# First products on a tile of ones, the sample's narrow products joined into longer turns, and the last unit's scaling on VectorE, in a streaming encoder layer

## The chip, the cores and the metric

The kernel runs on one core of one Trainium2 chip. The core's engines are TensorE (PE, matrix products; its weight loads are shown as PEld), VectorE (DVE), ScalarE (ACT), GpSimd (POOL) and SyncE (SP), which here only starts transfers. The metric is the device time of one execution in microseconds (us).

## The reference

One layer of an encoder is applied to two groups of rows that share all weights: a prompt of 2048 rows and a sample of 32 rows (the next frames of a running stream), each row of 1024 numbers, all in float32.

```python
h = rmsnorm(x, g_pre_mix)
z = h @ w_in                                  # 1024 -> 2560: u | q | f | i | g
u_ext = concatenate([pool_hist, u])           # mixer A: trailing means over 2, 4, 8, 16 frames
y_pool = einsum('blgc,gcd->blgd', d, w_pool) * pool_scale
S1, o = hgrn_run(S0, silu(zq), kin, zi, logf) # mixer B: 4 heads of 128, a gated recurrence
y_hg = rmsnorm(o, g_hg_norm) * silu(zg)
x = x + rmsnorm(concatenate([y_pool, y_hg]) @ w_out, g_post_mix)
h2 = rmsnorm(x, g_pre_ffn)
f = (silu(h2 @ w_gate) * (h2 @ w_up)) @ w_down   # 1024 -> 2816 -> 1024
x = x + rmsnorm(f, g_post_ffn)
```

Outputs are both groups' rows, and for each group the last 15 rows of u and the recurrence's final state.

## The kernel before

**Stages.** The prompt is worked on in two halves of 1024 rows; the second half carries the sample with it. For each half come the value columns (`first_values` for the first half, `values` for the second), four heads (`head_products`, with the recurrence in the generator `hgrn`), four pool columns (`pool_products`), the output projection (`project`, with `post` behind it), and gate and up (`gate_up`). When both halves are through, `down` makes the last product for both and writes the rows.

**Products.** A prompt product is made from parts in a rounded format: each operand is split into a high and a low part, and three products of 128x512 (high by high, high by low, low by high) are added up in one bank of PSUM. Twelve such products make one channel tile of four row tiles in `value_products`, or one slot in gate and up and in down, which use a seven-product scheme of two-by-two blocks. There are eight banks: four in the pool `mm` and four in the pool `ax`.

**Sample products.** The sample's 32 rows are multiplied in plain float32, with the sample as the stationary operand: 32 columns wide, so that four products stand side by side in the four column quarters of the array, and the k-th part of the sum goes to the quarter k mod 4. A product of four quarters is turned and summed by one more product with a 0/1 matrix (columns `C_I4` of the constants). The profile shows every plain float32 product as two records. Three kinds matter here:

- `fps`, in `sample_tile` (L618): eight products for one column tile of w_in, 16 records. They are issued as soon as the tile's weights are taken, ahead of the tile's prompt products; 5 us later by the planner's clock the copy `fst` is turned.
- `gb`, in `group` inside `hgrn` (L709): the small products within chunks of the recurrence, also 32 columns wide, in six groups for each head.
- `gsps`, in `sampled` (L1217): 16 products for one matrix tile pair of gate or up (32 records), issued right after product 6 of that tile. Even m is gate, odd m is up; a gate and an up tile share a bank, which `sample_hidden` (L1122) copies whole to `sT`, turns by four products `zps` with 32 columns, and multiplies to the hidden sample rows.

**Order.** PE's order is the order in which the code issues its products, with small tasks put in between: a `Task` holds a generator and a time on a counter (`Pace.t`) that every product advances by an estimate; `poll` steps each task whose time has come. In `gate_up` and `down` the slots are listed by `order_of`. Other engines' orders are made by a scheduler from the dependences. In `gate_up`, raw weight tiles (`wraw`) are loaded about nine slots ahead of use; `drop` frees a tile when its last part has been formed and, in the second half, when its sample products are made. A load that wants a buffer waits for that in SP's queue.

**The start.** `first_values` (L517) loads x by channels and the weights of the value columns. ScalarE forms the scaled high part `xg` (L532) and rounds the weights to `whw` (L213); VectorE forms the low parts (L533, L214). The first pass over the second row group uses the unscaled rows; `token_stats` (L422) computes for each row tile a sum of squares (ACT, L288), the reciprocal root (POOL, L294 and L295) and a diagonal matrix `dg` (POOL, L429), which `scaled_channels` (L449) multiplies with a matrix of ones into `rb`, for the second pass.

**The end.** In `down`, `half_done` (L1457) is called when one half (512 columns) of a row tile's sum is complete: square sum (ACT), scaling by g_post_ffn, and, after the second half, the reciprocal root. `done` finishes the row tile and stores it. For the very last unit (`direct`, row tiles 11 and 15) POOL multiplies three of the four halves by g_post_ffn (L1474), DVE the fourth (`fg`, L1471), DVE scales by the root and adds the residual (L1487), and stores go by SP and ACT queues.

## Time and profile before

| | us |
|---|---|
| median of 3 runs (lowest to highest) | 2156.44 (2155.46 to 2156.99) |
| the profiled execution's own time | 2157.55 |
| its span in the trace | 2155.7 |
| PE busy in the span | 2131.6 |
| DVE, ACT, POOL busy | 1426.7, 822.8, 286.3 |

The profile is one execution. The page gives busy time per engine, groups of instructions by line, and what ended the idle time before them; the list of waits says who waited for whom; the time-ordered view prints each instruction with its start and length from the span's start. Since products are pipelined, a 128x512 product is shown 0.39 us long although the next starts 0.23 us after it: cost is read from start to start.

### The profile page before, as it was taken

Reading aid. Unit: us, or ns where it says so; the run is one execution under the profiler, and the core shown is the slowest. Engines: PE = TensorE matmul, PEld = TensorE weight load, DVE = VectorE, ACT = ScalarE, POOL = GpSimd, SP = SyncE. Lnnn points to the kernel's source line nnn. Section 1 sums busy time; section 2 is a strip of 40 time slices with the busy share of each in tenths; the row PEclk is TensorE's granted clock in tenths of the full one; section 3 lists DMA queues with packets and bytes.
Section 4 is the critical chain, followed back from the end, with each engine's and each line's share of the span. In section 5 each row is a group of like instructions: output and inputs, shape, how many; then the busy total and the mean of one; then the engine's idle time right before and its main releaser. Section 6 shows DMA issues by size and latency. Waiting matters only on the chain.

```text
span 2155.7 us, 34195 instructions
## 1 busy us (share of the span) xinstructions
PE 2131.6 (99%) x13196; PEld 1702.8 (79%) x13196; DVE 1426.7 (66%) x2321; ACT 822.8 (38%) x1604; POOL 286.3 (13%) x391
## 2 busy tenths in 40 slices
PE   8999999999999999999999999999999999999998
PEld 6788778888888887777777788888888777877876
DVE  5655665787776777465574687766667756466587
ACT  6434345554444444233323564444434521011032
POOL 2233301100000010122220210000000211110134
PEclk9999999999999999999999999999999999999999
DMA  8121134445545559011004624544454796776778
GB/s 312 50 70 41 40 128 156 127 117 167 160 144 156 147 161 291 20 44 42 17 23 159 198 81 125 149 137 143 137 150 139 233 324 194 225 222 192 220 214 211
DMA packets 388783, 316.16 MB, mean 147 GB/s; under 512 B 16007, under 2 KB 318335, under 8 KB 388622
## 3 DMA queue, kind: packets, MB, share of 16 engines
q1 hardware_dynamic: 386318, 306.37, 46.6%
q0 software_dynamic: 2016, 7.34, 1.8%
q8 instruction: 104, 1.70, 0.3%
q14 instruction: 57, 0.47, 0.1%
q10 hardware_dynamic: 288, 0.28, 0.0%
HBM read 215.56 MB, written 98.37 MB: 146 GB/s over the span
## 4 chain that ended last, share of the span: by engine, by line
PE 89%; DVE 4%; ACT 1%; issue 1%; POOL 1%; DMA 1%; SPq 0%; DVEq 0%; POOLq 0%; ACTq 0%
PE gx L176 21%; PE mmb L176 15%; PE gy L176 11%; PE dx L176 10%; PE ops L176 9%; PE dy L176 5%; PE gz L176 5%; PE dz L176 2%; PE vps L176 2%; PE gb L176 1%; PE gsps L176 1%; PE gw L176 1%; PE ups L176 1%; DVE acc L1455 1%; PE pps L176 1%
## 5 line engine op out<-in xcount | busy, mean ns | idle before, releaser
L176 PE MATMUL gx<-fhi,wf 128*128 128x512 f32 x1376 | 447.5, 394 | 0.0
L176 PEld LDWEIGHTS gx<-fhi,wf 128*128 128x128 f32 x1376 | 258.4, 188 | 60.0 <-issue 1.0
L176 PE MATMUL gx<-flo,wf 128*128 128x512 f32 x688 | 269.8, 392 | 0.0
L176 PE MATMUL gy<-fhi,wf 128*128 128x512 f32 x704 | 232.8, 393 | 0.0
L176 PE MATMUL mmb<-hThi,whi 128*128 128x512 f32 x512 | 219.3, 428 | 0.0
L176 PE MATMUL dx<-dhi,hst 128*128 128x512 f32 x640 | 213.4, 394 | 0.4 <-DVE acc L1455 0.3
L176 PE MATMUL mmb<-hThi,wlo 128*128 128x512 f32 x512 | 201.8, 394 | 0.0
L176 PE MATMUL mmb<-hTlo,whi 128*128 128x512 f32 x512 | 201.6, 394 | 0.0
L1455 DVE TENSOR_TENSOR acc<-dx,acc 128x512 f32<-128x512 f32 x168 | 115.2, 689 | 77.1 <-PE dx L176 76.3
L1189 DVE TENSOR_TENSOR wf<-s,wf 128x512 fp32r<-128x512 f32 x176 | 120.4, 687 | 65.9 <-ACT wf L1184 63.1
L176 PEld LDWEIGHTS gy<-fhi,wf 128*128 128x128 f32 x704 | 132.1, 188 | 30.7 <-issue 0.2
L176 PEld LDWEIGHTS gx<-flo,wf 128*128 128x128 f32 x688 | 129.4, 188 | 28.4
L1184 ACT CAST wf<-s 128x512 fp32r<-128x512 f32 x176 | 108.2, 621 | 104.9 <-PE gy L176 34.9
L176 PEld LDWEIGHTS dx<-dhi,hst 128*128 128x128 f32 x640 | 120.1, 188 | 32.5 <-issue 3.4
L176 PE MATMUL gy<-flo,wf 128*128 128x512 f32 x352 | 137.9, 392 | 0.0
L176 PE MATMUL dx<-dlo,hst 128*128 128x512 f32 x320 | 125.8, 393 | 0.0
L1189 DVE TENSOR_TENSOR wf<-wraw,wf 128x512 fp32r<-128x512 f32 x132 | 89.5, 687 | 45.9 <-ACT wf L1184 45.7
L176 PEld LDWEIGHTS mmb<-hThi,whi 128*128 128x128 f32 x512 | 96.7, 189 | 25.2 <-issue 6.4
L176 PEld LDWEIGHTS mmb<-hThi,wlo 128*128 128x128 f32 x512 | 96.4, 188 | 22.4
L176 PE MATMUL dy<-dhi,hst 128*128 128x512 f32 x320 | 112.9, 393 | 0.3 <-DVE acc L1455 0.3
L1184 ACT CAST wf<-wraw 128x512 fp32r<-128x512 f32 x132 | 80.7, 621 | 82.5 <-PE gz L176 23.5
L176 PEld LDWEIGHTS mmb<-hTlo,whi 128*128 128x128 f32 x512 | 96.9, 189 | 18.5 <-issue 2.6
(332 smaller groups left out, 4102.9 us busy)
## 6 DMA issues: line engine op xcount, KB each, us to landing
hst<-hdFalse SPq DMA_DIRECT2D x140, 256.0 KB, 3.0
hst<-hdTrue SPq DMA_DIRECT2D x140, 256.0 KB, 3.1
wraw<-in_w_gate_dram SPq DMA_DIRECT2D x50, 512.0 KB, 4.2
wraw<-in_w_up_dram SPq DMA_DIRECT2D x50, 512.0 KB, 4.2
hdFalse<-hhi SPq DMA_DIRECT2D x77, 256.0 KB, 2.3
hdFalse<-hlo SPq DMA_DIRECT2D x77, 256.0 KB, 2.5
hdTrue<-hhi SPq DMA_DIRECT2D x77, 256.0 KB, 2.5
hdTrue<-hlo SPq DMA_DIRECT2D x77, 256.0 KB, 3.3
```

What stands on the lines that cost most here:

```text
L176: nc.tensor.matmul(out, l, r, start=start, stop=stop, skip_group_check=more)
L1184: nc.scalar.copy(wf[:, 0], getattr(M, src) if isinstance(src, str) else src)
L1189: nc.vector.tensor_tensor(wf[:, 1], getattr(M, src) if isinstance(src, str) else src, wf[:, 0].bitcast(F32), ALU.subtract)
L1455: nc.vector.tensor_tensor(dst, ps, dst, ALU.add)
```

## The change

1. `first_values` begins with a tiny activation on ACT and 12 products of a tile of ones by itself into a spare bank, which nothing reads.
2. The first channel tile's 12 products are ordered high by high, low by high, high by low over all four row tiles, instead of the three for each row tile in turn.
3. `token_stats` can do some of its row tiles; the first row group's four are done two and two in the second pass. `dg` is formed by DVE instead of POOL.
4. `sample_tile` becomes a task that begins 6.5 us later by the planner's clock, or when `join` calls it: `group` calls `join` just ahead of its own products, so that `fps` stands beside `gb`.
5. `sampled` takes a list. For gate tiles from m = 6 on, the sample products of gate and up are issued together after the gate tile's product 5 (after product 6 of the up tile for the last pair); the first six tiles are as before. The two matrix parts of a tile now share 128 columns of the bank (two quarters each), so that the copy is 256 wide instead of 512, and two products with 64 columns (constants `C_PAIR`) turn it instead of four with 32.
6. In the last unit DVE multiplies all four halves by g_post_ffn and POOL does both root steps; row tile 15 is finished one slot after its sum, and each row tile's second half is stored by ACT's queue.
7. The square sums of the second half's rows (`later_stats`) start 20 us later by the planner's clock.

The diff, cut to its core:

```diff
+    c[:, C_PAIR:C_END] = ((q[:, None] == r[None, :] // NS) & (s[:, None] == r[None, :] % NS)).astype(np.float32)
...
+        def token_stats(S, tg, tiles=range(4)):
...
-                nc.gpsimd.tensor_scalar(S.dg[tg][:, i], ident, S.rs[tg][i], None, ALU.mult)
+                nc.vector.tensor_scalar(S.dg[tg][:, i], ident, S.rs[tg][i], None, ALU.mult)
...
+            idle = small("idle", [P, 1], bufs=1)
+            nc.scalar.activation(idle, ones[:, 0:1], AF.Copy)
+            bank = axbank("idle")
+            for _ in range(12):
+                mm(bank[:, 0:P], ones, ones, True, True, 0.0)
...
-                    for i in range(4):
-                        value_products(pss, i, ah, al, i * P, hi[kk], lo[kk], k + kk == 0, k + kk == KD - 1)
+                    if k + kk == 0:
+                        for n, (a, b) in enumerate(((ah, hi[0]), (al, hi[0]), (ah, lo[0]))):
+                            for i in range(4):
+                                mm(pss[i], a[:, i * P:(i + 1) * P], b, n == 0, False, rcost(512))
+                    else:
...
                 if k == 2:
+                    token_stats(S, 0, range(2))
                     next(later, 0)
                 elif k == 4:
-                    token_stats(S, 0)
+                    token_stats(S, 0, range(2, 4))
...
-            ps = axbank("fps")
-            for k in range(KD):
-                q = k % 4
-                mm(ps[32 * q:32 * q + 32, 0:P], S.hsr[:, k, :], raw[:, k * P:(k + 1) * P], k < 4, k >= 4, 60.0)
-
-            def rest():
+
+            def whole():
+                task.begun = True
+                ps = axbank("fps")
+                for k in range(KD):
+                    q = k % 4
+                    mm(ps[32 * q:32 * q + 32, 0:P], S.hsr[:, k, :], raw[:, k * P:(k + 1) * P], k < 4, k >= 4, 60.0)
...
-            return Task(rest())
+            task = Task(whole(), 6500.0)
+            task.begun = False
+            Pace.joint.append(task)
+            return task
+
+        def join():
+
+            for tk in Pace.joint:
+                if not tk.begun:
+                    tk.step()
+            Pace.joint.clear()
...
             def group(goff, src, pick, n=16):
+                join()
...
-            st = t2("sT")
-            nc.vector.tensor_copy(st, sps)
+            st = t2("sT", [P, 2, P])
+            nc.vector.tensor_copy(st, sps[:, 0:2 * P].rearrange("p (m c) -> p m c", c=P))
...
-            for c in range(4):
-                mm(zps[:, c * NS:(c + 1) * NS], st[:, c * P:(c + 1) * P], cons[:, C_I4:C_I4 + NS], True, True, 215.0)
+            for c in range(2):
+                mm(zps[:, c * 2 * NS:(c + 1) * 2 * NS], st[:, c], cons[:, C_PAIR:C_END], True, True, 215.0)
...
-                    sampled(m, M)
+                    if m < LEAD or m == len(mats) - 1:
+                        sampled([m] if m < LEAD else [m - 1, m])
...
+                    if LEAD <= m < len(mats) - 2 and m % 2 == 0:
+                        sampled([m, m + 1])
...
-                if direct and dh == 1 and t == units[-1][2] + 8:
+                if direct:
                     fg = t2("fg")
                     nc.vector.tensor_tensor(fg, f, gpf[0][:, cs], ALU.mult)
-                    stats[t].append(fg)
-                elif direct:
-                    nc.gpsimd.tensor_tensor(f, f, gpf[0][:, cs], ALU.mult)
+                    stats[t].append((dh, fg))
...
-                    rstd_of(st, P, True, nc.vector if direct else nc.gpsimd, dh)
-                    pending.append((slot[0] + (0 if direct else 4), lambda: done(t, direct)))
+                    rstd_of(st, P, True, nc.gpsimd, dh)
+                    pending.append((slot[0] + (1 if direct else 4), lambda: done(t, direct)))
...
-                    Task(later_stats(halves[1]), 5000.0)
+                    Task(later_stats(halves[1]), 25000.0)
```

Three places in the orders. First PE in the first head of the second half, at the gate column's sample products: `fps` are the column tile's products, `mmb` the prompt's, `gb` the chunk products. Before:

```order
L176 MATMUL fps<-wraw,hsr 32x128 x8
L176 MATMUL mmb<-hThi_7375,whi 128x512
L176 MATMUL mmb<-hTlo_7376,whi 128x512
L176 MATMUL mmb<-hThi_7375,wlo 128x512
L176 MATMUL mmb<-hThi_7377,whi 128x512
L176 MATMUL mmb<-hTlo_7378,whi 128x512
L176 MATMUL mmb<-hThi_7377,wlo 128x512
L176 MATMUL mmb<-hThi_7379,whi 128x512
L176 MATMUL mmb<-hTlo_7380,whi 128x512
L176 MATMUL mmb<-hThi_7379,wlo 128x512
L176 MATMUL gb<-q_t,k_t 32x16 x33
```

And now:

```order
L180 MATMUL mmb<-hTlo_7395,whi 128x512
L180 MATMUL mmb<-hThi_7394,wlo 128x512
L180 MATMUL fps<-wraw,hsr 32x128 x8
L180 MATMUL gb<-q_t,k_t 32x16 x33
L180 MATMUL mmb<-hThi_7396,whi 128x512
```

The column tile's products have moved behind nine prompt products, to the edge of the chunk products. Of 16 column tiles eight stand beside a `gb` now, one before (another stood beside the value columns' sample products `vsps` before, and no longer does).

Second PE in gate and up of the second half, at a gate tile of the steady part: `gx` are prompt products, `gsps` the sample's. Before, after the gate tile's product 6:

```order
L176 MATMUL gx<-fhi,wf 128x512 x2
L176 MATMUL gx<-flo,wf 128x512
L176 MATMUL gx<-fhi,wf 128x512
L176 MATMUL gsps<-wraw,hs_11306 32x128 x16
L176 MATMUL gz<-fhi,wf 128x512
```

And now, after its product 5:

```order
L180 MATMUL gx<-fhi,wf 128x512 x2
L180 MATMUL gx<-flo,wf 128x512
L180 MATMUL gx<-fhi,wf 128x512
L180 MATMUL gsps<-wraw,hs_11321 32x128 x32
L180 MATMUL gx<-fhi,wf 128x512
```

The up tile's 16 products have come to the gate tile's. In all, turns of 32-column products on PE (one or more of `fps`, `gb`, `gsps` and the others in a row) are 96 before and 82 now.

Third DVE at the end: `acc` are the row sums, `dx`, `dy`, `dz` banks of the last unit's products, `fg` the halves multiplied by g_post_ffn (`gv`), `x1r` the residual. Before:

```order
L1455 TENSOR_TENSOR acc<-dz,acc 128x512
L1490 SCALAR_TENSOR_TENSOR acc<-acc,st,gv 128x512
L1455 TENSOR_TENSOR acc<-dy,acc 128x512
L1455 TENSOR_TENSOR acc<-dx,acc 128x512
L1455 TENSOR_TENSOR acc<-dy,acc 128x512
L1455 TENSOR_TENSOR acc<-dx,acc 128x512
L292 TENSOR_SCALAR st<-st 128x1
L1471 TENSOR_TENSOR fg<-acc,gv 128x512
L1487 SCALAR_TENSOR_TENSOR acc<-acc,st,x1r 128x512 x2
L292 TENSOR_SCALAR st<-st 128x1
L1487 SCALAR_TENSOR_TENSOR acc<-acc,st,x1r 128x512
L1487 SCALAR_TENSOR_TENSOR acc<-fg,st,x1r 128x512
```

And now:

```order
L1526 SCALAR_TENSOR_TENSOR acc<-acc,st,gv 128x512
L1509 TENSOR_TENSOR fg<-acc,gv 128x512
L1493 TENSOR_TENSOR acc<-dy,acc 128x512
L1493 TENSOR_TENSOR acc<-dx,acc 128x512
L1509 TENSOR_TENSOR fg<-acc,gv 128x512
L1493 TENSOR_TENSOR acc<-dy,acc 128x512
L1509 TENSOR_TENSOR fg<-acc,gv 128x512
L1493 TENSOR_TENSOR acc<-dx,acc 128x512
L1523 SCALAR_TENSOR_TENSOR acc<-fg,st,x1r 128x512
L1509 TENSOR_TENSOR fg<-acc,gv 128x512
L1523 SCALAR_TENSOR_TENSOR acc<-fg,st,x1r 128x512 x3
```

A product `fg` has come ahead of the first add of `dy`, two more stand between the adds, and the two small root steps have left DVE for POOL.

More of the change, by code (lines that the diff above doesn't have):

```diff
@@ L44 @@
 C_VEC = C_I4 + NS
-C_END = C_VEC + 32
+C_PAIR = C_VEC + 32
+C_END = C_PAIR + 2 * NS
 NPAIR = NJ // 2
@@ L116, in body @@
         w_down = ins["w_down"][0]
-        vec = cons[:, C_VEC:C_END]
+        vec = cons[:, C_VEC:C_PAIR]
         g_pre, g_ffn, p_scale, g_hg = vec[:, 0:8], vec[:, 8:16], vec[:, 16:20], vec[:, 28:29]
@@ L170, in body @@
             tasks = []
+            joint = []
         def tick(ns):
@@ L1142, in gate_up @@
                 S.hsm = ztile("hsm", [P, NJ, NS])
-            jobs, later = [], []
+            jobs, later, gs = [], [], {}
             def load(m, p):
@@ L1486, in done @@
                     if direct:
-                        nc.vector.scalar_tensor_tensor(f[:, ds], fg[0] if fg and i else f[:, ds], rs, xh[:, ds], ALU.mult, ALU.add)
-                        (nc.scalar if fg and i else nc.sync).dma_start(out=outs[0][0, rows, ds], in_=f[:, ds])
+                        nc.vector.scalar_tensor_tensor(f[:, ds], dict(fg)[i], rs, xh[:, ds], ALU.mult, ALU.add)
+                        (nc.scalar if i else nc.sync).dma_start(out=outs[0][0, rows, ds], in_=f[:, ds])
                     else:
```

42 lines of the change are left out of this document (25 added, 17 removed).

## The prediction

> **What bounds the kernel now.** I read the profile page first, then the list of waits of TensorE, then the time-ordered view of the first 30 us, of one turn of each kind of sample product, and of the last 15 us. The first fence is the busy line of the page and two rows of the waits (engine, operation waited with, releaser: us in total, times, longest).
>
> ```profile
> PE 2131.6 (99%) x13196; PEld 1702.8 (79%) x13196; DVE 1426.7 (66%) x2321; ACT 822.8 (38%) x1604; POOL 286.3 (13%) x391
> ...
> PE vps L176 <- ACT whw L213: 6.8, 1, 6.8
> PE rb L176 <- POOL dg L429: 1.1, 1, 1.1
> ```
>
> TensorE (PE) is busy for 2131.6 of 2155.7 us. Of the 24.1 us left, 6.85 are the wait for the first weights, some 10 lie behind the last product, and the largest other wait that the change touches is 1.1 us. So the time is the length of the queue of products, plus its two ends. A change pays if it shortens that queue or one of the ends, and costs if it opens a new wait in the queue. Other engines matter only there.
>
> **The start.** First half of the time-ordered view (start, length, engine, line, operation, out<-in, count, idle before).
>
> ```profile
> 0.77 0.20 POOL L137 MEMSET ones<- 128x128 f32 x1
> ...
> 4.27 1.28 ACT L532 ACT_TABLE_LOAD   x1 [4.27 <-DMA xT<-x_channels]
> ...
> 6.20 1.12 ACT L213 CAST whw<-wrow 128x512 fp32r<-128x512 f32 x2
> ...
> 6.85 0.79 PE L176 MATMUL vps<-whw,xg 128*128 128x512 f32 x1 [6.85 <-ACT whw L213]
> ...
> 12.16 1.00 PE L176 MATMUL vps<-whw,xg 128*128 128x512 f32 x2
> ...
> 13.00 0.39 PE L176 MATMUL vps<-wlw,xg 128*128 128x512 f32 x1
> 13.23 0.63 PE L176 MATMUL vps<-whw,xg 128*128 128x512 f32 x2
> ...
> 20.86 0.19 ACT L288 ACTIVATION_READ_ACCUMULATOR junk<-xt 128x1 f32 x1
> ...
> 26.58 1.05 PE L176 MATMUL rb<-dg,ones 128*128 128x128 f32 x8
> ...
> 27.39 0.47 PE L176 MATMUL vps<-whw,xg 128*128 128x512 f32 x1
> ```
>
> Two products from 12.16 to 13.00 are 0.42 us each; from 13.00 to 13.23 one takes 0.23. So the first 6 us of products run at half rate, and then the full rate is granted. From 6.85 to the rb products at 26.58 stand six channel tiles of 12 products, 72 in 19.73 us; at 0.23 they would take 16.6, so 3.1 us are lost to the slow beginning.
>
> The change puts 12 products of a tile of ones (24 records) ahead. They can start when that tile is set, at about 1.0. The eight rb records take 0.81 us (26.58 to 27.39), 0.10 each; at half rate 0.20, so 24 end at about 5.9. The table load also moves from 4.27 to the idle activation at about 1.2, so the first weight cast could start 1.28 earlier, at 4.9, if its data were there; they landed at 6.20 at the latest. The first real product therefore falls between 5.6 and 6.85; I take 6.1, just behind the idle ones. With full rate from there, rb comes at 6.1 + 16.6 = 22.7 instead of 26.58: 3.9 us. I take off 0.4 for a rest at half rate: **3.5 us**, between 1.5 (the rate rises late) and 4.2. The Trainium skill, page "TensorE: Matmul & The Clock Gate", section "What's actually happening", says that the full rate needs one busy window of about 3.4 us and that these windows run freely. The trace agrees as far as it can: 6 us of half rate lie within one to two windows. By that rule the full rate would come anywhere from 4.4 to 7.8, at worst 1.7 us of half rate after 6.1, which costs 0.9 instead of my 0.4.
>
> The new order of the first 12 products (four with the low weight part last) only takes away the need for wlw as the second operand. The square sums that feed the first rb stay where the landing of their rows puts them; the last ends at 21.05, and two POOL steps (the longer, the power, takes 0.54 in a row of the end below) and dg on VectorE (DVE) then end at about 22.2, just ahead of rb at 22.7. If they came later, they would take from the 3.5. In the second pass two of four sums are brought forward, and dg no longer queues on POOL, so the 1.1 us wait of the second rb should go: **1.1**, between 0 and 1.1.
>
> **The sample products.** Three kinds of turn of PE in the second half. In each fence stand the last full product ahead, the turn, and the two products behind it (one in the third). First a turn of the gate and up products, 32 records; then a turn of one column tile, 16 records; then the one place where a column tile already stands beside the chunk products (gb).
>
> ```profile
> 1279.58 0.39 PE L176 MATMUL gx<-fhi,wf 128*128 128x512 f32 x1
> 1279.90 1.08 PE L176 MATMUL gsps<-wraw,hs 128*32 128x128 f32 x32
> 1280.91 0.50 PE L176 MATMUL gx<-fhi,wf 128*128 128x512 f32 x1
> 1281.24 0.39 PE L176 MATMUL gx<-flo,wf 128*128 128x512 f32 x1
> ```
>
> ```profile
> 881.71 0.39 PE L176 MATMUL mmb<-hThi,wlo 128*128 128x512 f32 x1
> 882.02 0.64 PE L176 MATMUL fps<-wraw,hsr 128*32 128x128 f32 x16
> 882.60 0.50 PE L176 MATMUL mmb<-hThi,whi 128*128 128x512 f32 x1
> 882.93 0.39 PE L176 MATMUL mmb<-hTlo,whi 128*128 128x512 f32 x1
> ```
>
> ```profile
> 907.72 0.39 PE L176 MATMUL mmb<-hThi,wlo 128*128 128x512 f32 x1
> 908.04 0.77 PE L176 MATMUL gb<-qa,k_t 128*32 128x16 f32 x66
> 908.71 0.64 PE L176 MATMUL fps<-wraw,hsr 128*32 128x128 f32 x16
> 909.29 0.51 PE L176 MATMUL mmb<-hThi,whi 128*128 128x512 f32 x1
> ```
>
> Cost of a turn: from the product ahead to the second behind, less two products of 0.23. For 32 records 1281.24 - 1279.58 - 0.46 = 1.20; for 16 records 882.93 - 881.71 - 0.46 = 0.76. So a record is 0.0275 us and a turn has a fixed 0.32 to 0.34 us whatever it holds: 0.08 more ahead, 0.10 behind, the rest while the array empties. Eight pairs (seven in the steady part, and the last) now hold 64 records in one turn instead of twice 32: 8 x 0.34 = **2.7 us**, at least 8 x 0.18 = 1.4 if only the two edges go.
>
> In the order of PE, turns of narrow products fall from 96 to 82: these eight, and six column tiles fewer that stand alone (14 before, 8 now). In the last fence gb goes into fps without an edge: fps still takes 0.58 to the next product as it does alone. So a join saves the edges, 0.18, and up to 0.34 if one emptying goes as well. I take 0.2: 6 x 0.2 = **1.2**, up to 2.0.
>
> The turn of the sample's hidden rows, now four products with 32 moving columns (8 records):
>
> ```profile
> 1290.50 0.97 PE L176 MATMUL zps<-cons,sT 128*128 128x32 f32 x8
> 1291.31 0.48 PE L176 MATMUL gy<-fhi,wf 128*128 128x512 f32 x1
> ```
>
> 0.81 us for 8 records, 0.10 each, as much as an rb record with 128 columns. So width does not set it up to 128, and four records with 64 columns take 0.40: 11 pairs x 0.405 = **4.5**. The trace has no record of 64 columns; if each took twice as long nothing would be gained, but the rb row speaks for 4.5.
>
> **The end.** The last operations (the last product of all starts at 2145.28).
>
> ```profile
> 2142.63 0.50 PE L176 MATMUL dy<-dhi,hst 128*128 128x512 f32 x1 [0.34 <-DVE acc L1455]
> ...
> 2144.33 0.69 DVE L1455 TENSOR_TENSOR acc<-dy,acc 128x512 f32<-128x512 f32 x1 [0.96 <-PE dy L176]
> ...
> 2145.28 0.40 PE L176 MATMUL dx<-dhi,hst 128*128 128x512 f32 x1
> ...
> 2146.51 1.26 POOL L1474 TENSOR_TENSOR acc<-acc,gv 128x512 f32<-128x512 f32 x1
> 2146.64 1.68 DVE L1471 TENSOR_TENSOR fg<-acc,gv 128x512 f32<-128x512 f32 x1
> ...
> 2147.74 1.01 POOL L295 TENSOR_TENSOR st<-st,nhalf 128x1 f32<-128x1 f32 x1
> ...
> 2150.40 0.54 POOL L295 TENSOR_TENSOR st<-st,nhalf 128x1 f32<-128x1 f32 x1 [1.65 <-DVE st L292]
> ...
> 2151.64 0.75 DVE L1487 SCALAR_TENSOR_TENSOR acc<-fg,st,x1r 128x512 f32<-128x512 f32 x1
> 2152.43 0.35 ACTq L1488 DMA_DIRECT2D out_dram<-acc  x1
> ```
>
> Beside POOL's product DVE's own takes 1.68 where an add takes 0.69, and POOL's power waits for POOL's product. Now DVE does all four products. One of them stands ahead of the add of dy that PE already waits for (0.34), so PE waits 0.65 longer and everything after is 0.65 later. Tile 15's add then ends at 2144.33 + 0.69 + 0.65 = 2145.67, its square sum (some 0.8) and two POOL steps (the power 0.54, the other shorter) at 2147.5. From there DVE has five operations of 0.7 (in the new order one scaling, one product, three scalings): 2151.0. Before it ended at 2151.64 + 0.75 = 2152.39. **1.4 us**, between 0.5 (the power takes 1.01 as in the row of 2147.74, with some queueing on DVE) and 2.4 (no delay of PE, shorter gaps). The final store follows as before.
>
> **The sum.** 3.5 + 1.1 + 2.7 + 1.2 + 4.5 + 1.4 = 14.4 us off the profiled execution's 2157.55, so 2143.1. That execution is 1.1 above the median of the runs, 2156.44, which becomes 2142.0. Smaller edits go at nothing: sT is copied at half its width on DVE, which PE does not wait for there; dg on DVE is eight short operations in a stretch where DVE waits for PE; one more of the last stores goes out by ScalarE's (ACT) queue, empty by then; and the square sums of the second half's rows start 20 us later but are read only when that half begins.
>
> **Rivals.**
> *The array stays slow at the start* (12 per cent): the idle products do not raise the rate, or outlast the weights. Then 3.5 goes: 2145.5. For it: the trace has no such records in its first 6 us, so no row shows that they count as work; against it: the rate did rise after 6 us of products.
> *The fixed part does not go with the join* (8): each narrow product group empties the array anyway. Then 2.7 + 1.2 go: 2145.9. The third fence speaks against it.
> *New waits for banks in the heads and pool columns* (10): fps now begins beside gb, which holds two of four banks, and pool columns want one for every pps; a product waits up to 1 us at each of eight joins, 8 us lost: 2150.
> *Held weights* (3), the slower side. A gate tile's raw weights are now read three products of 12 later, 3 x 2.77 = 8.3 us, and loads wait for them in SyncE's (SP) queue, with the stores of the hidden rows behind them.
>
> ```profile
> SPq L227 <- PE gsps L176: 16.9, 13, 3.7
> ```
>
> ```profile
> wraw<-in_w_gate_dram SPq DMA_DIRECT2D x50, 512.0 KB, 4.2
> ```
>
> ```profile
> 1423.32 0.37 SPq L227 DMA_DIRECT2D wraw<-in_w_gate_dram  x1
> ...
> 1433.71 0.68 DVE L1159 TENSOR_TENSOR s<-wraw 128x512 f32<-128x512 f32 x1
> ```
>
> The fences are SP's waits (as above), the page's row of these loads (the last number is us to landing), and one load and the sum that first reads it. From load to first use 10.4 us, of which landing takes 4.2, so 6.2 us are spare. If all 8.3 fell on both loads of a gate, each would be 2.1 late, and if DVE's lead of five products (14 us) were used up too, 7 pairs x 2 x 2.1 = 29 us would be lost: 2171. It decides only where SP's waits for gsps pass 6.2 us; the longest is 3.7 now, and the sums stand 14 us ahead of PE.
>
> **The numbers.** The forecast has what is left, 67 per cent. Its low end is the largest terms (4.2, 1.1, 2.7, 2.0, 4.5, 2.4: 16.9, so 2139.5), with 1 us more for waits of PE that the shift in time removes; its high end takes in either of the first two rivals (2145.9) and 2 us of the lower bounds of the other terms, 2148; the last two rivals are left out. A measurement here tells 0.2 per cent, 4.3 us, from no change: faster means below 2152.1. Faster 0.92 (the forecast, the first two rivals, and half of the third's spread), same 0.05, slower 0.03.
>
> **What would show it.** At the start: idle records from 1.0 to about 6, vps records 0.39 long from the first, rb at about 22.7, and no wait of rb for dg. In the middle: gsps turns of 64 records that take about 2.06 by the same measure, zps turns of 0.40, fps beside gb. At the end: dy waiting about 1.0 for DVE, and DVE's last operation ending 5.1 us behind the start of the last product instead of 7.1. I am wrong if PE's wait list has a new row of over 2 us, or if a 64-record turn costs 2.4.

## The result, and the profile after

The kernel after takes 2145.39 us (median of 4 runs, 2143.87 to 2146.02), the kernel before 2156.72 beside it (2155.46 to 2158.26): a ratio of 0.9946, with a 95% interval of 0.9932 to 0.9961. It is 11.3 us faster, where 14.4 were forecast. The time lies 3.4 us above the forecast of 2142.0, which went by a median of 2156.44 before, and inside its range. The profiled execution took 2145.8 with a span of 2144.0.

The busy line of the page, and the three longest of TensorE's waits (engine, operation, releaser: us in total, times, longest):

```profile
PE 2124.1 (99%) x13176; PEld 1702.8 (79%) x13176; DVE 1431.6 (67%) x2330; ACT 822.0 (38%) x1605; POOL 281.6 (13%) x382
```

```profile
PE gb L180 <- ACT f_t L789: 2.5, 1, 2.5
PE gb L180 <- POOL k_t L757: 1.8, 1, 1.8
PE gb L180 <- DVE qa L758: 1.5, 1, 1.5
```

The wait for the first weights and that of the second rb are gone. Three waits of gb stand there instead, one of them longer than the 2 us that the prediction named as a sign of being wrong.

Since both kernels make the same products in the same stages, PE's queue can be cut at the same six products in both traces. The stretch between two of them tells what each part of the change did (us; "gained" is before less after):

| stretch | start in before | start in after | before | after | gained | forecast |
|---|---|---|---|---|---|---|
| start, to the first rb | 0 | 0 | 26.58 | 22.89 | 3.69 | 3.5 |
| to the first half's first gx | 26.58 | 22.89 | 364.25 | 364.23 | 0.02 | 1.1 |
| to the second half's first head product | 390.83 | 387.12 | 479.70 | 479.73 | -0.03 | 0 |
| to the second half's first gx | 870.53 | 866.85 | 364.65 | 365.13 | -0.48 | 1.2 |
| to the first dx | 1235.18 | 1231.98 | 467.17 | 460.14 | 7.03 | 7.2 |
| to the last product | 1702.35 | 1692.12 | 442.93 | 443.01 | -0.08 | -0.65 |
| from the last product to the end of the span | 2145.28 | 2135.13 | 10.42 | 8.87 | 1.55 | 2.05 |
| sum | | | 2155.70 | 2144.00 | 11.70 | 14.4 |

The big terms came as forecast. What is missing was lost in two stretches, both with heads and pool columns. The last two rows together gained 1.47, where 1.4 was forecast, though not quite in the way that was forecast.

**The start.** Time-ordered view (start, length, engine, line, operation, out<-in, count, idle before):

```profile
1.02 5.44 PE L180 MATMUL idle<-ones 128*128 128x128 f32 x24 [1.02 <-POOL cmps L145]
1.17 1.28 ACT L526 ACT_TABLE_LOAD   x1 [1.17 <-PEq L1680]
...
6.16 2.16 PE L180 MATMUL vps<-whw,xg 128*128 128x512 f32 x8
...
9.08 0.39 PE L180 MATMUL vps<-whw,xg 128*128 128x512 f32 x1
...
22.89 1.05 PE L180 MATMUL rb<-dg,ones 128*128 128x128 f32 x8
```

The idle records end where the weights come, at 6.16, and the first 12 products take 2.92 us (6.16 to 9.08); at 0.23 each they would take 2.76. So the full rate is there almost from the first real product: the granted clock is 1.00 from 6.29 on, where before had it from 12.97 on.

**The sample products in gate and up**, a joined turn and a turning one:

```profile
1416.42 0.40 PE L180 MATMUL gx<-fhi,wf 128*128 128x512 f32 x1
1416.75 1.95 PE L180 MATMUL gsps<-wraw,hs 128*32 128x128 f32 x64
...
1418.98 0.39 PE L180 MATMUL gx<-flo,wf 128*128 128x512 f32 x1
...
1426.86 0.39 PE L180 MATMUL gx<-fhi,wf 128*128 128x512 f32 x1
1427.09 0.55 PE L180 MATMUL zps<-cons,sT 128*128 128x64 f32 x4
...
1427.77 0.40 PE L180 MATMUL gx<-flo,wf 128*128 128x512 f32 x1
```

By the measure of the prediction (from the product ahead to the second behind, less 0.46) a turn of 64 records costs 1418.98 - 1416.42 - 0.46 = 2.10, where two of 32 cost 2.40: 0.30 to 0.33 is saved at each of eight. The two turning products (four records) cost 1427.77 - 1426.86 - 0.46 = 0.45, where the four of before (eight records) cost 0.90: a record of 64 columns takes no longer than one of 32.

**A column tile beside gb:**

```profile
892.91 0.39 PE L180 MATMUL mmb<-hThi,wlo 128*128 128x512 f32 x1
893.23 0.64 PE L180 MATMUL fps<-wraw,hsr 128*32 128x128 f32 x16
893.69 0.82 PE L180 MATMUL gb<-q_t,k_t 128*32 128x16 f32 x66
...
894.78 0.39 PE L180 MATMUL mmb<-hTlo,whi 128*128 128x512 f32 x1
```

Both together cost 894.78 - 892.91 - 0.46 = 1.41. A turn of fps alone costs 0.76, one of gb alone 0.89 by the same measure, so a join saves 0.24, a little more than the 0.2 that was put in.

**Where it was lost, first half.** gb of the last head waits for k_t. POOL's rows just ahead of it, and gb:

```profile
228.72 1.64 POOL L451 TENSOR_TENSOR st_b<-st_b,nhalf 128x8 f32<-128x8 f32 x1
230.31 1.30 POOL L757 TENSOR_TENSOR k_t<-k_t,tt 128x512 f32<-128x512 f32 x1
231.66 0.73 PE L180 MATMUL gb<-qa,k_t 128*32 128x16 f32 x64 [1.80 <-POOL k_t L757]
```

st_b are the reciprocal roots of the second half's rows, the step that edit 7 put off. They now stand directly ahead of the merge of k_t, and their power alone takes 1.64 us.

**Where it was lost, second half.** The pool columns: the first and the last of five wide operations of the window on DVE, then the merge's tt, the two copies on ACT that form f_t anew, and gb:

```profile
1068.47 1.24 DVE L941 TENSOR_TENSOR sa<-e_t 128x1038 f32<-128x1038 f32 x1
...
1074.80 1.23 DVE L943 SCALAR_TENSOR_TENSOR sa<-sb,e_t 128x1024 f32<-128x1024 f32 x1
...
1076.06 0.71 DVE L759 TENSOR_TENSOR tt<-f_t 128x528 f32<-128x528 f32 x1
...
1076.86 0.67 ACT L789 COPY f_t<-q_t 128x528 f32<-128x528 f32 x1 [1.81 <-DVE tt L759]
1077.43 0.66 ACT L789 COPY f_t<-qa 128x528 f32<-128x528 f32 x1
...
1078.23 1.18 PE L180 MATMUL gb<-f_t,k_t 128*32 128x32 f32 x66 [2.54 <-ACT f_t L789]
```

The merge's tt at 1076.06 reads f_t, which ACT then overwrites with its two copies; gb reads these. So ACT waits for tt, and gb for ACT, and tt stands behind all five wide operations.

The kernel before had waits in this stretch too, at other products, and they are all but gone in after:

```profile
PE ops L176 <- DVE S L845: 1.7, 1, 1.7
PE pps L176 <- DVE sa L915: 0.9, 1, 0.9
```

All waits of the stretch add up to 2.8 us in before and 5.1 in after. So 2.3 us of new waiting stand against seven joins of 0.24, 1.7 in all, which is about the 0.5 lost.

**The end.** DVE's and POOL's last rows, and dy:

```profile
2131.74 0.68 DVE L1493 TENSOR_TENSOR acc<-dy,acc 128x512 f32<-128x512 f32 x1
...
2132.47 0.50 PE L180 MATMUL dy<-dhi,hst 128*128 128x512 f32 x1 [1.03 <-DVE acc L1493]
...
2137.17 1.04 POOL L296 TENSOR_SCALAR st<-st 128x1 f32<-128x1 f32 x1 [0.40 <-ACT junk L292]
2137.47 0.69 DVE L1509 TENSOR_TENSOR fg<-acc,gv 128x512 f32<-128x512 f32 x1
...
2138.29 0.94 POOL L299 TENSOR_TENSOR st<-st,nhalf 128x1 f32<-128x1 f32 x1
2139.26 1.41 DVE L1523 SCALAR_TENSOR_TENSOR acc<-fg,st,x1r 128x512 f32<-128x512 f32 x2 [0.44 <-POOL st L299]
```

dy waits 1.03, as forecast. DVE's last operation ends at 2140.67, 5.54 behind the start of the last product instead of 5.1: the two root steps take 1.04 and 0.94 on POOL beside DVE, where 1.0 was put in for both, and DVE waits 0.44 for the second. The stretch ahead of the last product became only 0.08 longer although dy waits 0.69 more in it. Where the other 0.6 came from is not shown; the stretch is 442.93 in before and 443.54 in e6_paironly below, which has the same code there, so it moves by this much by itself.

### The profile page after: what moved, and what is told of

It reads as the page before. It is cut to its first block, busy times and chain, and to the rows that moved or that the text cites. A ratio compares the mean times of both kernels' runs of the same rounds, so it can differ in the third digit from the quotient of the medians.

```text
span 2144.0 us, 34134 instructions
## 1 busy us (share of the span) xinstructions
PE 2124.1 (99%) x13176; PEld 1702.8 (79%) x13176; DVE 1431.6 (67%) x2330; ACT 822.0 (38%) x1605; POOL 281.6 (13%) x382
## 4 chain that ended last, share of the span: by engine, by line
PE 82%; DVE 4%; ACT 1%; issue 1%; POOL 1%; DMA 1%; DVEq 0%; POOLq 0%; SPq 0%; ACTq 0%
PE gx L180 21%; PE gy L180 11%; PE dx L180 10%; PE mmb L180 10%; PE ops L180 9%; PE dy L180 5%; PE gz L180 4%; PE dz L180 3%; PE vps L180 2%; PE gw L180 1%; PE gsps L180 1%; PE gb L180 1%; DVE acc L1493 1%; PE ups L180 1%; PE pps L180 1%
```

## The experiments

The times of a kernel spread by 1.3 to 5.3 us, and the ratio's interval is about 0.15% to each side. So the terms of 0.5 to 3 us are read from the stretches of the traces, and the times are given beside them. Each run has one profile, and a stretch of the same code can differ by 0.6 us between two profiles, and by 1.4 where the granted clock differs (below).

| kernel | median us | before, same chip | ratio (95%) |
|---|---|---|---|
| e1_stats5 | 2145.07 | 2155.28 | 0.9953 (0.9938 to 0.9968) |
| e2_poolnow | 2142.60 | 2155.28 | 0.9940 (0.9925 to 0.9955) |
| e3_nojoin | 2144.76 | 2155.28 | 0.9949 (0.9932 to 0.9965) |
| e4_noidle | 2147.78 | 2155.28 | 0.9964 (0.9951 to 0.9977) |
| e5_sep | 2148.99 | 2156.42 | 0.9967 (0.9954 to 0.9980) |
| e6_paironly | 2152.07 | 2156.42 | 0.9980 (0.9970 to 0.9989) |
| e7_held | 2144.95 | 2156.42 | 0.9948 (0.9931 to 0.9964) |
| e8_best | 2140.28 | 2156.42 | 0.9926 (0.9911 to 0.9940) |
| a_again (after) | 2145.29 | 2155.93 | 0.9951 (0.9938 to 0.9963) |
| b_again (e8_best) | 2141.30 | 2155.93 | 0.9932 (0.9918 to 0.9945) |
| e9_oldorder | 2146.14 | 2155.93 | 0.9955 (0.9941 to 0.9968) |
| e10_poolfg | 2140.76 | 2156.60 | 0.9928 (0.9914 to 0.9941) |

**Edit 7 undone (e1_stats5).**

```diff
-                    Task(later_stats(halves[1]), 25000.0)
+                    Task(later_stats(halves[1]), 5000.0)
```

> The kernel after with edit 7 alone undone (the square sums of the second half's rows start 5 us instead of 25 us later by the planner's clock). After waits 1.8 us at 231.7, where gb waits for k_t of POOL, and 1.64 us of POOL's time just ahead of that k_t is the power of later_stats. Theory: that step has moved in front of the merge and makes the wait, so with 5 us the wait is under 0.3, nothing new comes in its place, and the time is 1.5 to 1.8 us shorter than after: about 2143.7. Rival: the power only fills a gap and k_t is late by itself; then a wait of 1 us or more stays there and the time is within 0.5 of after, 2145.4.

POOL's merge and gb in this kernel:

```profile
227.74 1.31 POOL L757 TENSOR_TENSOR k_t<-k_t,tt 128x512 f32<-128x512 f32 x1 [5.85 <-PE gb L180]
...
229.81 0.74 PE L180 MATMUL gb<-qa,k_t 128*32 128x16 f32 x64
```

The merge starts 2.6 us earlier and gb waits for nothing. The second stretch is 362.83 instead of 364.23, 1.4 us shorter, and 363.04, 362.76 and 363.01 in the three later profiles with this edit. The median does not show it: it came out at 2145.07, not at the 2143.7 of the theory, which its interval allows. The cause of the wait is shown by the trace; the gain in time alone would not have been.

**The column tiles (e2_poolnow, e3_nojoin).** The first begins the sample tiles of the pool columns at once, the second all sample tiles:

```diff
+            if smp:
+                smp.step()
```

```diff
-            Pace.joint.append(task)
+            task.step()
```

> The kernel after with the sample tiles of the pool columns begun at once as before; those of the heads still wait for gb. In after gb waits 2.5 us for f_t of ACT at 1078 and 1.5 us for qa of DVE at 1095, both in the second half's pool columns, and DVE's order there puts the 1024-wide adds of the windows ahead of the merge. Theory: the later turn of the sample tiles changed that order; with them begun at once DVE's order is that of before, the two waits fall from 4.0 to the 2.6 or less that before had there, two or so joins (0.25 each) are lost, and the time is 0.9 to 3.5 us shorter than after: about 2143.5. Rival: the waits come from the earlier start of the second half's heads as a whole, not from the sample tiles; then they stay at about 4.0 and the time is 0 to 0.5 us longer than after.

> The kernel after with all sample tiles of w_in begun at once as before (edit 4 undone; no fps stands beside gb through a join). Theory: by the turns of after (gb and fps together 1.41 us against 0.89 and 0.77 alone) six joins are lost, 1.5 us, and the waits of the pool columns shrink from 4.0 to 2.6 or less: the time is within 1.5 us of after, 2144.0 to 2146.9, so edit 4 as a whole gains nothing. Rival (the prediction's 1.2 alone, with no part in the waits): the waits stay and the time is 1.2 to 1.5 us longer than after, 2146.6 to 2146.9.

DVE, ACT and gb in the pool columns of e2_poolnow:

```profile
1069.18 1.24 DVE L943 TENSOR_TENSOR sa<-e_t 128x1038 f32<-128x1038 f32 x1 [0.25 <-ACT e_t L927]
...
1072.95 0.69 DVE L759 TENSOR_TENSOR tt<-f_t 128x528 f32<-128x528 f32 x1
...
1076.47 0.79 PE L180 MATMUL gb<-f_t,k_t 128*32 128x32 f32 x66
```

tt stands behind two wide adds instead of five operations, and gb's wait of 2.54 is gone; one of 1.8 for qa is left (4.0 in all in after, 1.8 in both kernels here). So the order on DVE that the turn of the sample tiles made is the cause. The fourth stretch is 361.18 instead of 365.13. About 1.3 of these 3.95 us are the clock, below; the rest, 2.6, is the waits, which fell from 5.1 to 2.0 in the stretch, less a lost join. One join is lost, not two (eight tiles stand beside gb in after, seven here, two in e3_nojoin). In gate and up a wait of gy of 1.0 came up here, which is 0.2 at most in the three later profiles with this edit.

In e3_nojoin the waits are 1.8 as well, but the stretch is 363.79. Against e2_poolnow that is 2.6 more, of which the clock makes up at most 1.7 (it is 0.50 for 3.41 us from 1094.48 on); 0.9 or more is left for five joins, at least 0.18 each, where the turns give 0.24. With its time within 0.6 of after, edit 4 as it stands gains nothing that can be measured: what its joins bring, its order on DVE takes. The rival that the waits have nothing to do with it is out.

**The start (e4_noidle, e9_oldorder).** Without the idle products, and with the first 12 products in the old order:

```diff
-            bank = axbank("idle")
-            for _ in range(12):
-                mm(bank[:, 0:P], ones, ones, True, True, 0.0)
```

```diff
-                    if k + kk == 0:
-                        for n, (a, b) in enumerate(((ah, hi[0]), (al, hi[0]), (ah, lo[0]))):
...
+                    for i in range(4):
+                        value_products(pss, i, ah, al, i * P, hi[kk], lo[kk], k + kk == 0, k + kk == KD - 1)
```

> The kernel after without the 12 products of ones; the tiny activation, which brings the table load forward, stays, and so do all other edits. Theory: the idle products buy the full rate. Without them the first 6 us of real products run at half rate, which loses 3.0 us; the table load alone brings the first product from 6.85 to about 6.2. So rb stands at about 25.9 instead of 22.9 and the time is 3.0 us longer than after: 2148.4. Rival: the gain of 3.7 at the start comes from the order of the first 12 products and the table load; then rb stands at 23 to 24 and the time is within 1 us of after.

> The kernel after with edit 2 alone undone: the first 12 products in the old order, three for each row tile. In after the first low weight part is formed on VectorE from 6.07 to 6.7; in the old order the second product needs it. Theory: the second product waits for it, about 0.3 us, at 6.4 to 6.7, and the rest runs at full rate; so edit 2 is worth 0.3 us, rb stands at 23.2, and the 1.8 us of the start that the idle products do not explain are the earlier table load and the length of the slow stretch. Rival: the wait lowers the granted clock again, and rb stands 1 us or more later, 23.9 or more.

The first products without the idle ones:

```profile
5.89 3.78 PE L180 MATMUL vps<-whw,xg 128*128 128x512 f32 x8 [5.89 <-ACT whw L217]
9.47 1.70 PE L180 MATMUL vps<-wlw,xg 128*128 128x512 f32 x4
11.01 0.40 PE L180 MATMUL vps<-whw,xg 128*128 128x512 f32 x1
```

Twelve products take 5.12 us (5.89 to 11.01), and rb stands at 24.82: in this pair of profiles the idle products are worth 1.93 of the 3.69 us (2.34 against the second profile of after, whose rb stands at 22.48), neither the 3.0 of my theory nor nothing, as the rival had it. This size is not fixed. The full clock is granted 4.91 us behind the first product here, 6.12 in before, and 4.39 in e6_paironly, which starts as before does; the time until then runs at half rate, so 2.2 to 3.1 us are lost. In the ten profiles of kernels that start as after does, the full clock comes between 4.15 and 7.14, and rb stands between 22.48 and 23.39.

In the old order the second product waits 0.38 for the low weight part, and rb stands at 23.19. The theory said 23.2, but this lies within the range of those ten, so the place of rb alone shows nothing. From the first product to rb it is 17.34; in the four profiles with the new order in which, as here, the full clock comes ahead of the first product (a_again, e5_sep, e8_best, e10_poolfg) it is 16.65 to 16.71. So the order is worth 0.6 to 0.7, about twice the theory's 0.3, by one profile. The table load moved from 4.27 to 1.17 and brings the first weights from 6.85 to 5.89, 0.96. These three make 3.5 of the 3.69.

**The turns of gate and up (e5_sep, e6_paironly).** Each tile's sample products by themselves in the kernel after, and the pair's layout alone in the kernel before:

```diff
-                    if m < LEAD or m == len(mats) - 1:
-                        sampled([m] if m < LEAD else [m - 1, m])
+                    sampled([m])
...
-                    if LEAD <= m < len(mats) - 2 and m % 2 == 0:
-                        sampled([m, m + 1])
```

```diff
...
-            for c in range(4):
-                mm(zps[:, c * NS:(c + 1) * NS], st[:, c * P:(c + 1) * P], cons[:, C_I4:C_I4 + NS], True, True, 215.0)
+            for c in range(2):
+                mm(zps[:, c * 2 * NS:(c + 1) * 2 * NS], st[:, c], cons[:, C_PAIR:C_END], True, True, 215.0)
...
```

> The kernel after with the sample products of each gate and up tile issued by themselves, right after that tile's product 6, as before (layout and turning of the pair as in after). Theory: a turn of the array costs a fixed 0.32, so eight turns more (22 of 32 records instead of 8 of 64 and 6 of 32) cost 8 x 0.32 = 2.6 us, all of them between the first product of gate and up and the first of down: 2.6 us longer there and 2.6 longer in all than after. Rival: only the edges, 0.18, go with a join and the rest of the 2.6 came from weights held longer or loads that moved; then the stretch is 1.4 us longer.

> The kernel before with the pair's layout alone: the two matrix parts share 128 columns, sT is 256 wide, and two products with 64 moving columns (4 records) turn it instead of four with 32 (8 records); everything else as before. Theory: a record's time is set by its 128 stationary columns, so 11 turns fall from 0.89 to 0.44 us and the time is 11 x 0.45 = 4.9 us shorter than before. Rival (two sides): a record with 64 columns takes twice as long as one with 32, and nothing is gained; or the copy of half the width on VectorE is worth something too, and more than 5.5 is gained.

In e5_sep the stretch from gx to dx is 462.13 instead of 460.14, and no wait is in it. The eleven profiles with after's products in this stretch take 459.54 to 459.95 without their waits (after 459.94), so the eight turns more cost 2.2 to 2.6 us. The turns, 22 at 1.21 against 6 at 1.21 and 8 at 2.09, give 2.6. The rival's 1.4 is out. The median is 3.6 above that of after, where 2.6 was expected, but its five executions lie 5.3 apart. In e6_paironly the stretch falls from 467.17 to 463.08, by 4.1, with a new wait of gy of 0.4 in it; the time falls by 4.35, with an interval of 2.4 to 6.5. The turns alone give 4.95. The rival's gain of more than 5.5 lies within the interval of the time; the stretch excludes it. That a record of 64 columns costs as much as one of 32 is shown by the turns (0.90 to 0.45, in all 11); some 0.4 of the gain was lost beside that wait, and where stays open.

**The end, and a version that beats both (e7_held, e8_best, e10_poolfg).** e7_held issues the first product with g_post_ffn one slot later. e8_best joins this with the edits of e1_stats5 and e2_poolnow. e10_poolfg has those two, but gives that one product to POOL:

```diff
-                    nc.vector.tensor_tensor(fg, f, gpf[0][:, cs], ALU.mult)
+                    def scaled():
...
+                    if len(seen) == 1:
+                        held.append(scaled)
...
```

```diff
+                    eng = nc.gpsimd if len(stats) == 15 and len(seen) == 1 else nc.vector
+                    eng.tensor_tensor(fg, f, gpf[0][:, cs], ALU.mult)
```

> The kernel after with one step of the last unit put off: the product of the first half with g_post_ffn on VectorE is issued one slot later, behind the add of dy that TensorE waits for. Theory: the wait of dy falls from 1.03 to 0.3 to 0.4, the last product starts 0.65 earlier, and the tail behind the last product keeps its length (5.5 us to the end of VectorE's last operation): 0.65 us less in all, which shows in the trace and hardly in the times. Rival: VectorE is full there, so the put-off product delays the next add instead and dy or dx waits 0.6 somewhere else; then the end does not move.

> The kernel after with three edits together: the square sums of the second half's rows as before (5 us), the sample tiles of the pool columns begun at once, and the last unit's first product put off by one slot. Theory: the 1.8 us wait for k_t, the 2.5 us wait for f_t and 0.65 of the wait of dy go, and the two joins of the pool columns (0.5) are lost: 1.7 + 2.3 + 0.65 = 4.6 us less than after, in spans from 2144.0 to about 2139.4. Rival: the gains are not additive, since waits in the gate and up stretch (as the 1.0 of gy with the sample tiles begun at once) take up the shift; then 3 us or less.

> The kernel with the square sums of the second half's rows as before and the sample tiles of the pool columns begun at once, as in the combination, but with the last unit's first product with g_post_ffn given back to POOL instead of put off on VectorE. Putting it off cut the wait of dy from 1.03 to 0.43 but lengthened the tail from 5.54 to 6.02 us, since VectorE is full there. Theory (VectorE's queue bounds the last 8 us): with one operation of 0.69 less, dy waits 0.3 to 0.4 and VectorE's last operation ends 5.5 us or less behind the start of the last product: 0.5 us less from the first product of down to the end than in the combination, about 2140. Rival (POOL bounds it): POOL's product takes 1.3 to 1.7 us beside VectorE and delays its root steps; then the tail is 6 us or more.

dy and DVE's last rows in e7_held, then POOL's product and the same rows in e10_poolfg:

```profile
2131.84 0.50 PE L180 MATMUL dy<-dhi,hst 128*128 128x512 f32 x1 [0.43 <-DVE acc L1493]
...
2134.25 1.29 DVE L1510 TENSOR_TENSOR fg<-acc,gv 128x512 f32<-128x512 f32 x2
...
2139.08 1.41 DVE L1528 SCALAR_TENSOR_TENSOR acc<-fg,st,x1r 128x512 f32<-128x512 f32 x2 [0.71 <-POOL st L299]
```

```profile
2124.68 0.73 DVE L1529 SCALAR_TENSOR_TENSOR acc<-acc,st,gv 128x512 f32<-128x512 f32 x1
2124.84 1.71 POOL L1512 TENSOR_TENSOR fg<-acc,gv 128x512 f32<-128x512 f32 x1 [0.60 <-DVE acc L1495]
...
2126.07 0.50 PE L180 MATMUL dy<-dhi,hst 128*128 128x512 f32 x1 [0.36 <-DVE acc L1495]
...
2132.84 1.41 DVE L1526 SCALAR_TENSOR_TENSOR acc<-fg,st,x1r 128x512 f32<-128x512 f32 x2 [0.44 <-POOL st L299]
```

In e7_held the last product starts 0.66 earlier within its stretch (442.35 instead of 443.01), but DVE now has two products ahead of its last add, and its last operation ends 6.02 behind the start of the last product instead of 5.54. Of the 0.66 some 0.2 is left: the theory fell, and the rival, that DVE is full there, was right, though the cost came in the tail and not as another wait of dy or dx. With one operation less on DVE, e10_poolfg keeps both: dy waits 0.36, the last product starts at 2128.70 and DVE's last operation ends at 2134.25, 5.55 behind. From the first product of down to the end of the span that is 0.45 less than in e8_best (450.69 and 451.14), where 0.5 was expected. So the order of DVE's queue makes the wait of dy, and moving all four products to it was one too many. The tail did not get shorter than after's with one operation less on DVE: it is 5.55 and 5.54, and DVE waits 0.44 for POOL's root step in both. So DVE is not all that sets the last 5.5 us; the root steps on POOL stand in the same chain, and the theory that DVE's queue alone bounds the end is not shown.

e8_best takes 2140.28, e10_poolfg 2140.76. The profiled span of e8_best, 2137.7, is 6.3 below that of after, where 4.6 was expected; the clock accounts for 1.4 of it (below). On one chip after took 2145.29 and e8_best 2141.30, 4.0 less, where 4.6 to 6 were expected; the intervals of the two ratios overlap (0.9938 to 0.9963 and 0.9918 to 0.9945), which the expectation had denied. The five executions of each do not overlap, 2144.32 to 2146.72 against 2139.91 to 2142.08, and the profiled spans, 2142.9 and 2138.1, are 4.8 apart. e8_best and e10_poolfg are not to be told apart by their times.

**What moves the times by 1.4 us (a_again, b_again).**

> The kernel after once more, as the measure for the next one on the same chip. Both theories: 2143.9 to 2146.0 as before. It also tests what moved the times by 1 to 2 us between kernels that differ in nothing near there: theory, the granted clock falls for 2 to 4 us behind the longest wait of the second half in some executions and not in others, and costs 1.4 us when it does; then the spans of this kernel fall into two groups about 1.4 us apart, those at mean clock 0.999 the shorter. Rival: the spans spread evenly, and the clock has no part in it.

> The kernel with three edits together (square sums of the second half's rows as before, sample tiles of the pool columns begun at once, the last unit's first product put off) once more beside after on the same chip. Theory: 4.6 to 6 us shorter than after on the same chip, 2139.5 to 2140.8, with the intervals of the ratios to before apart. Rival: the 4.6 us between two chips' runs were chance, and it is under 3 us here.

The same wait of 2.5 us, the products behind it, and a row that sums up 1078 to 1082, in the two profiles of the kernel after (the third number from the end of that row is the granted clock):

```profile
1078.23 1.18 PE L180 MATMUL gb<-f_t,k_t 128*32 128x32 f32 x66 [2.54 <-ACT f_t L789]
...
1080.35 0.63 PE L180 MATMUL mmb<-hThi,wlo 128*128 128x512 f32 x1
1080.78 0.63 PE L180 MATMUL mmb<-hThi,whi 128*128 128x512 f32 x1
...
1078.00:1082.00 4.00, 3.77 (x73) 3.27 (x74) 3.33 (x6) 1.12 (x3) 1.77 (x1) 0.57 0.02 4
```

```profile
1078.30 0.78 PE L180 MATMUL gb<-f_t,k_t 128*32 128x32 f32 x66 [2.53 <-ACT f_t L789]
...
1079.59 0.39 PE L180 MATMUL mmb<-hThi,wlo 128*128 128x512 f32 x1
1079.82 0.40 PE L180 MATMUL mmb<-hThi,whi 128*128 128x512 f32 x1
...
1078.00:1082.00 4.00, 3.70 (x78) 2.89 (x78) 3.40 (x6) 1.19 (x3) 1.49 (x1) 1.00 0.01 4
```

In the first, gb takes 1.18 instead of 0.78 and the products behind it come 0.43 apart instead of 0.23; the granted clock is 0.57 from 1078 to 1082 in the mean (0.50 from 1078.07 to 1081.48), and 1.00 in the second. Seven profiles have this wait and these products. In four (after, e1_stats5, e7_held, e9_oldorder) the clock falls behind it, and the fourth stretch takes 365.00 to 365.29; in three (a_again, e4_noidle, e5_sep) it does not, and the stretch takes 363.72 to 363.82. So a wait of 2.5 us can cost 3.9.

What decides is where it falls. In every trace the clock changes only at whole multiples of 3.41 us from the moment of the first full clock, and it stays at half for one such stretch. In the four profiles 2.1 to 2.5 us of the wait lie within one stretch; in the three it is split into two parts of 1.2 to 1.4 us. Where the stretches begin differs from execution to execution, and that part is chance. The kernel before loses such a stretch too, from 1118.88 on behind its wait of 1.72, so the table's row compares like with like.

The expected two groups of whole spans did not show: in a_again they are 2142.5 and 2142.9 at a mean clock of 0.999, and 2143.4, 2144.6 and 2144.9 at 0.998. The clock orders them, but other stretches add to it.

## Why the prediction was right, and where it was not

- *The start, 3.5:* measured 3.69, right in size, and in part by luck. The reason holds: the idle products bring the full clock forward. But how much that is worth depends on when the clock is granted without them, 6.1 us behind the first product in the profile that the prediction read, 4.9 and 4.4 in two others, so 3.1, 2.5 or 2.2 us; and the order of the first products, which the prediction put at nothing, is worth 0.6 to 0.7.
- *The second rb, 1.1:* the wait went, as forecast, but the stretch did not get shorter. The failing step is among the edits that "go at nothing": the later square sums, because they "are read only when that half begins". It looked at who reads the result, and not at what the step comes to stand in front of on POOL's queue: a power of 1.64 us ahead of the merge that gb waits for. e1_stats5 shows it.
- *gsps, 2.7, and zps, 4.5:* measured 2.6 and 4.95 by the turns, 7.0 together in their stretch, so 0.5 less than the turns add up to. The mechanism was right in both; the prediction's own rows give 0.32 for a turn's fixed part, where it took 0.34.
- *fps, 1.2:* the joins are there, but the stretch lost 0.5. The failing step is that the prediction counted edges of PE and asked only whether banks would be free. The later turn of the pool columns' tiles changed DVE's order, and gb waited 2.5 for it. e2_poolnow and e3_nojoin show it.
- *The end, 1.4:* 1.55 in the tail, less the added wait of dy (1.03 instead of 0.34), so 0.86 by its own rows. The wait was right; the root steps on POOL beside DVE, put in at 1.0, took 2.0. That the last two rows of the table come to 1.47 is luck.
- *The rivals.* The array did not stay slow (12 per cent), and the fixed part went (8 per cent). The third, new waits in the heads and pool columns (10 per cent), is the one that came in part: not for banks but for operands of three engines, with 3.5 us more waiting in the two stretches than before (the rb wait left out) instead of 8. Its sign in the prediction, "a new row of over 2 us", is in the list; that the time still fell inside the range is due to the larger terms.

Held weights, the rival on the slower side, did not decide, but came near it. The loads' waits for gsps in SP's queue, in after:

```profile
SPq L231 <- PE gsps L180: 29.0, 8, 5.3
```

The longest is 5.3 us now instead of 3.7, still under the 6.2 from which, by the prediction's estimate, it would have cost something, and gate and up got 7.0 shorter.

## What to carry to other kernels

A step that nobody reads for a long time is not free to move: ask what stands behind it on its engine at its new place. Where a scheduler sets the order of an engine, moving a product on PE may reorder work elsewhere that PE waits for, so a change of edges on PE is costed with the waits of the same stretch. And where times spread as much as the terms, cutting PE's queue at the same products in both traces tells terms of about 1 us apart, once the granted clock in the stretch has been looked at: the same products took 363.8 or 365.1 us here in two executions of one kernel.

## What the runs showed of the hardware

- A wait of 1.7 us can halve the granted clock for 3.41 us, which costs up to 1.7 us. Between the first full clock and the last product this happened eight times in the fourteen profiles. Each time TensorE had been idle for at least 1.72 us of one of the stretches of 3.41 us between which the clock can change: 1.72 in before, 1.77 in e6_paironly, 1.79 in e3_nojoin and, at 233.46, in e9_oldorder, 2.1 to 2.5 in the other four. With 1.71 (after, at 231.57) or less it never happened; with 1.78 to 1.80 it also failed to happen three times (e2_poolnow twice, e8_best). The Trainium skill, page "TensorE: Matmul & The Clock Gate", section "Why this matters for your kernels", advises to avoid gaps of more than about 3 us; these rows differ, shorter ones are enough.
- An operation with two operands in SBUF on DVE and one on POOL do not share time, the later one waits: in e10_poolfg POOL's product takes 1.71 beside DVE's scaling that began 0.16 earlier, against 1.26 without such a neighbour ahead of it in before. The Trainium skill, page "SBUF — State Buffer", section "SBUF: two separate sides", states this as a lock for the whole instruction; the trace agrees. The same fits the root steps at the end of after: 1.04 and 0.94 while DVE ran a product with gv and scalings with x1r, which have two operands in SBUF, against 0.27 and 0.56 from 2135.86 on, while DVE added from a PSUM bank (one operand in SBUF) or stood still.
- A plain float32 product of 128 stationary columns took about 0.1 us a record at 32, 64 and 128 moving columns (zps 0.90 for eight records, 0.45 for four; rb 0.81 for eight).
